# Instance norm on one core: the stores of the first two parts go from ScalarE's DMA queue to SyncE's

## The chip, the cores and the metric

The kernel runs on one core of one Trainium2 chip. The metric is device time in microseconds. Three runs of the kernel before took 1247.9, 1248.1 and 1248.12 us, median 1248.1. A core has five engines that matter here: TensorE (PE in the profile), VectorE (DVE), ScalarE (ACT), GpSimd (POOL) and SyncE (SP). SP and ACT each issue transfers on a hardware queue of their own; the profile names SP's queue q1 and ACT's q10. Both queues are worked off by the same 16 DMA engines.

## The reference

```python
# x: (8, 64, 32, 64, 64) float32, eps = 1e-5
mean = np.mean(x, axis=(2, 3, 4), keepdims=True)
var = np.var(x, axis=(2, 3, 4), keepdims=True)
return ((x - mean) / np.sqrt(var + eps)).astype(np.float32)
```

There are 512 instances (batch times channel) of 131072 float32 each, 268.4 MB in and as much out. Each instance is normalised by its own mean and variance.

## The kernel before

**Tiles and parts.** The input is one flat run of floats. A *part* is 128 partitions by 4096 floats, that is four whole instances, 2.1 MB, with 16 KiB in a partition. A *tile* is 128 by 12288 floats (three chunks of 4096), twelve instances, 6.3 MB, 48 KiB in a partition. The first two parts of the data (FRONT = 2) are done as parts, then come 41 tiles, then three more parts: 2 + 41 x 3 + 3 = 128 parts in all. Four slots of a tile's size hold the data (`slots[0]` to `slots[3]`); everything is computed in place in them.

**Where parts lie.** The two front parts use the first 4096 columns of slots 2 and 3, so the tile loads into slots 2 and 3 must wait until these parts have been stored. The three end parts lie side by side in slot 1, and are loaded when the store of tile 37, the last but three, has landed. The last tile, number 40, lies in slot 0.

**What is computed.** For a tile, VectorE and ScalarE sum the chunks, TensorE adds the sums over the partitions of an instance by a matrix of 1/131072 under a mask, a few small VectorE instructions (`over_instance`) put them together, and the same is done for the squares of the centred values; then VectorE scales two chunks and ScalarE one. For a part the same is done with one chunk, half of the elementwise work on each engine. The engines work through the parts and tiles in order: front parts, tiles, end parts (`over_tiles`). Each step is ordered by semaphores, one of each kind per slot or part ("lane"): `landed` (load done), `done` (scaled values ready), `stored` (store landed) are the ones that matter here.

**What sets the order of transfers.** There is no scheduler: each engine's instructions run in the order in which the code writes them, and one that waits holds up all that is behind it on the same engine.

- SP issues all loads (`load_all`): the two front parts, the tiles into slots 0 and 1, then those into slots 2 and 3, which wait for the stores of the first and second front part, then a loop over tiles 4 to 39 (line 391), each of which waits for the store of the tile four before it, then tile 40 (line 396) and the three end parts. Behind all of them SP stores tile 40 (line 402) and the three end parts (line 407).
- ScalarE issues the stores of tiles 0 to 39 (line 243) and, in the kernel before, those of the two front parts (line 310), each right behind the activation that finishes the data, in its own stream of instructions.

Which queue carries what, before: q1 has all loads, the last tile's store and the end parts' stores; q10 has the stores of the front parts and of tiles 0 to 39.

Of the kernel before, what the change touches and what calls it, by code (L numbers as in the profile page):

```python
# [9 lines left out]
def kernel(  # L10
# [26 lines left out]
    FRONT = 2  # L37
# [6 lines left out]
    out_f = out.rearrange("b c d h w -> (b c d h w)")  # L44
# [7 lines left out]
    def part_of(ap, m):  # L52
        first = (m if m < FRONT else m + THIRDS * n_tiles) * P * CHUNK
        return ap[first : first + P * CHUNK].rearrange("(p f) -> p f", p=P)
# [26 lines left out]
    def semaphores(name, n=LANES):  # L81
        return [ctx.enter_context(nc.semaphore(f"{name}{i}")) for i in range(n)]
# [11 lines left out]
    done = semaphores("done")  # L94
    stored = semaphores("stored")
# [188 lines left out]
            op1=Alu.add,  # L284
        )._wait_ge(shifted[lane], 1).then_inc(done[lane], 1)

    def part_on_scalar(eng, t, lane, dst):
        a, w = small[lane], CHUNK // 2
        eng.activation(  # L289
            out=unused[0][:, :w], in_=t[:, w:], func=Act.Identity, accum_out=a[:, 1:2]  # L290
        )._wait_ge(landed[lane], 16).then_inc(summed[lane], 1)
        eng.activation(  # L292
            out=unused[1][:],
            in_=t,
            func=Act.Square,
            bias=a[:, 2:3],
            accum_out=a[:, 3:4],
        )._wait_ge(centred[lane], 1).then_inc(squared[lane], 1)
        eng.activation(  # L299
            out=a[:, 5:6], in_=psum[lane][:, 2:3], func=Act.Sqrt, bias=eps_t[:, 0:1]  # L300
        )._wait_ge(varied[lane], 1).then_inc(rooted[lane], 1)
        eng.activation(  # L302
            out=t[:, :w],
            in_=t[:, :w],
            func=Act.Identity,
            scale=a[:, 6:7],
            bias=a[:, 7:8],
        )._wait_ge(shifted[lane], 1).then_inc(done[lane], 1)
        if dst is not None:
            eng.dma_start(out=dst, in_=t)._wait_ge(done[lane], 2).then_inc(  # L310
                stored[lane], 16
            )

    def part_on_tensor(eng, t, lane):
        a, p = small[lane], psum[lane]
# [9 lines left out]
    parts = [  # L325
        (SLOTS + m, slots[SLOTS - FRONT + m][:, :CHUNK], SLOTS - FRONT + m, 0)
        for m in range(FRONT)
    ]
# [14 lines left out]

    def over_tiles(eng, on_part, on_tile, with_target=False):
        def part(m):
            more = (part_of(out_f, m) if m < FRONT else None,) if with_target else ()
            on_part(eng, parts[m][1], parts[m][0], *more)

        for m in range(FRONT):
            part(m)  # L350
        counts = [
            ctx.enter_context(eng.register(f"{on_tile.__name__}_c{m}"))
            for m in (1, 3, 4, 16)
        ]
        for c, m in zip(counts, (1, 3, 4, 16)):
            eng.reg_mov(c, m)
        with eng.Fori(0, ROUNDS) as it:
            for s in range(SLOTS):
                more = (out_t[it * SLOTS + s],) if with_target else ()
                on_tile(eng, slots[s][:], s, *counts, *more)  # L360
            for c, m in zip(counts, (1, 3, 4, 16)):
                eng.reg_add(c, c, m)
        for k in range(ROUNDS * SLOTS, n_tiles):
            c = k // SLOTS + 1
            more = (out_t[k],) if with_target else ()
            if with_target and k == TAIL:
                more = (None,)
            on_tile(eng, slots[k % SLOTS][:], k % SLOTS, c, 3 * c, 4 * c, 16 * c, *more)
        for m in range(FRONT, n_parts):
            part(m)  # L370

    def load_all(eng):
        def part(m):
            lane, t, slot, uses = parts[m]
            load = eng.dma_start(out=t, in_=part_of(x_f, m))
            if uses:
                load._wait_ge(stored[slot], 16 * uses)
            load.then_inc(landed[lane], 16)

        for m in range(FRONT):  # L380
            part(m)
        for s in range(SLOTS):
            load = eng.dma_start(out=slots[s][:], in_=x_t[s])
            if s >= SLOTS - FRONT:
                load._wait_ge(stored[s + FRONT], 16)
            load.then_inc(landed[s], 16)
        c16 = ctx.enter_context(eng.register("load_c16"))
        eng.reg_mov(c16, 16)
        with eng.Fori(1, ROUNDS) as it:
            for s in range(SLOTS):  # L390
                eng.dma_start(out=slots[s][:], in_=x_t[it * SLOTS + s])._wait_ge(  # L391
                    stored[s], c16
                ).then_inc(landed[s], 16)
            eng.reg_add(c16, c16, 16)
        for k in range(ROUNDS * SLOTS, n_tiles):
            eng.dma_start(out=slots[k % SLOTS][:], in_=x_t[k])._wait_ge(
                stored[k % SLOTS], 16 * (k // SLOTS)
            ).then_inc(landed[k % SLOTS], 16)
        for m in range(FRONT, n_parts):
            part(m)  # L400
        s = TAIL % SLOTS
        eng.dma_start(out=out_t[TAIL], in_=slots[s][:])._wait_ge(
            done[s], 3 * (TAIL // SLOTS + 1)
        ).then_inc(stored[s], 16)
        for m in range(FRONT, n_parts):
            lane, t, _, _ = parts[m]
            eng.dma_start(out=part_of(out_f, m), in_=t)._wait_ge(done[lane], 2).then_inc(
                stored[lane], 16
            )

        for s in range(SLOTS):
            eng.wait_ge(stored[s], 16 * len(range(s, n_tiles, SLOTS)))
        for m in range(FRONT, n_parts):
            eng.wait_ge(stored[SLOTS + m], 16)

    def set_up(eng):
# [56 lines left out]
        return count  # L473

    load_all(nc.sync)
    set_by = set_up(nc.gpsimd)
    nc.vector.wait_ge(ready, set_by)
# [3 lines left out]
    nc.scalar.preload_act_table(Act.Sqrt)  # L481
    nc.scalar.wait_ge(ready, set_by)
    over_tiles(nc.scalar, part_on_scalar, tile_on_scalar, with_target=True)


# [33 lines left out]
```

## Time and profile before

| | |
|---|---|
| median of three runs | 1248.1 us (1247.9 to 1248.12) |
| the profiled execution, its own time | 1247.9 us |
| its span in the profile | 1246.2 us |
| moved | 536.9 MB, half in and half out, 431 GB/s over the span |
| VectorE busy | 804.6 us (65%) |
| ScalarE busy | 764.6 us (61%) |
| TensorE busy | 55.0 us (4%) |
| tile loads (41), median from issue to landing | 39.9 us |
| tile stores on ACT's queue (40), median from issue to landing | 54.2 us |
| part stores on ACT's queue (2), median | 27.9 us |
| part stores on SP's queue (3), median | 19.5 us |

The span is the stretch from the first to the last recorded instruction of the profiled execution; the time of an execution is some 1.7 us longer. A line of the timeline reads: start in us, length in us, engine, line of the code, operation, what is written and read, count, and in brackets the idle time before it and what ended that. An engine with a "q" (SPq, ACTq) is the engine's issuing of a transfer, not the transfer. "Issue to landing" runs from the issue of a DMA to the moment at which all 16 DMA engines have reported its data there; it holds the time that the transfer waits behind others on its queue.

### The profile page before, as it was taken

How to read it: one execution, taken by the hardware profiler on the slowest of the kernel's cores; microseconds unless marked ns; L12 is line 12 of the kernel's file. 1: busy time of each engine (PE TensorE's matmuls, PEld its weight loads, DVE VectorE, ACT ScalarE, POOL GpSimd, SP SyncE). 2: the span in 40 equal slices, each digit the busy share in tenths (PEclk: the TensorE clock that was granted, in tenths of full speed). 3: DMA queues.
4: the chain of work that ended last, by engine and by line, in shares of the span. 5: the costliest groups of instructions: out<-in, count | busy, mean ns of one | idle time of the engine just before them, and what ended most of it. 6: DMA issues, size and time to landing. Idle time of an engine off the chain costs nothing.

```text
span 1246.2 us, 1977 instructions
## 1 busy us (share of the span) xinstructions
PE 55.0 (4%) x184; PEld 46.1 (4%) x184; DVE 804.6 (65%) x722; ACT 764.6 (61%) x441; POOL 2.7 (0%) x15
## 2 busy tenths in 40 slices
PE   0000000000000000000000000000000000000000
PEld 0000000000000000000000000000000000000000
DVE  2887666666666666666666666666666666666661
ACT  5876555666566666655556665666566555566574
POOL 0000000000000000000000000000000000000000
DMA  9999999999999999999999999999999999999998
GB/s 395 429 429 439 440 429 432 431 426 448 432 429 429 432 443 435 429 431 432 440 439 429 429 432 437 442 431 429 431 431 448 432 429 429 432 442 439 430 422 368
DMA packets 13250, 536.89 MB, mean 431 GB/s; under 512 B 1472, under 2 KB 1472, under 8 KB 1472
## 3 DMA queue, kind: packets, MB, share of 16 engines
q1 hardware_dynamic: 7200, 281.02, 52.3%
q10 hardware_dynamic: 6048, 255.86, 47.4%
q14 instruction: 2, 0.02, 0.0%
HBM read 268.44 MB, written 268.44 MB: 431 GB/s over the span
## 4 chain that ended last, share of the span: by engine, by line
another core or an unknown queue 82%; DMA 9%; ACT 3%; DVE 2%; SPq 1%; issue 1%; PE 0%; ACTq 0%
DMA slot<-in_x_dram 6%; DMA out_dram<-slot 4%; ACT unused L222 1%; SPq L391 1%; ACT unused L292 1%; DVE small L159 0%; ACT unused L215 0%; DVE slot L202 0%; DVE slot L195 0%; ACT slot L302 0%; PE psum L253 0%; DVE small L266 0%; ACT unused L289 0%; PE psum L316 0%
## 5 line engine op out<-in xcount | busy, mean ns | idle before, releaser
L215 ACT ACTIVATE unused<-slot 128x4096 uint8<-128x4096 f32 x82 | 243.5, 2970 | 302.4 <-DMA slot<-in_x_dram 300.1
L159 DVE TENSOR_REDUCE small<-slot 128x1 f32<-128x4096 f32 x82 | 249.2, 3081 | 272.4 <-DMA slot<-in_x_dram 272.4
L222 ACT ACTIVATE unused<-slot,small 128x4096 uint8<-128x4096 f32 x82 | 303.5, 3703 | 63.6 <-DVE small L145 63.6
L173 DVE CUSTOM_DVE_ANT_0 unused<-slot 128x4096 uint8<-128x4096 f32 x41 | 181.5, 4426 | 1.4
L235 ACT ACTIVATE slot<-slot,small 128x4096 f32<-128x4096 f32 x41 | 155.9, 3802 | 18.1 <-DVE small L190 18.1
L202 DVE TENSOR_SCALAR slot<-slot,small 128x4096 f32<-128x4096 f32 x41 | 98.7, 2408 | 0.0
L253 PE MATMUL psum<-small,avg 128*128 128x9 f32 (+1 forms) x164 | 49.1, 375 | 1116.5 <-DVE small L127 1116.5
L166 DVE TENSOR_SCALAR slot<-slot,small 128x4096 f32<-128x4096 f32 x41 | 96.5, 2353 | 1.5
L195 DVE TENSOR_SCALAR slot<-slot,small 128x4096 f32<-128x4096 f32 x41 | 96.3, 2348 | 0.0
L253 PEld LDWEIGHTS psum<-small,avg 128*128 128x128 f32 x164 | 41.1, 311 | 1124.5 <-DVE small L127 1124.5
L133 DVE TENSOR_REDUCE small<-psum 128x3 f32<-128x12 f32 x82 | 13.9, 169 | 56.6 <-PE psum L253 56.6
L229 ACT ACTIVATE small<-small,eps_t 128x3 f32<-128x3 f32 x41 | 12.3, 300 | 61.2 <-DVE small L145 61.2
L127 DVE TENSOR_TENSOR small<-small,belongs 128x12 f32<-128x12 f32 x82 | 13.9, 170 | 31.3 <-ACT unused L222 28.9
L292 ACT ACTIVATE unused<-slot,small 128x4096 uint8<-128x4096 f32 x5 | 18.5, 3709 | 6.0 <-DVE small L269 6.0
L266 DVE TENSOR_REDUCE small<-slot 128x1 f32<-128x2048 f32 x5 | 11.4, 2283 | 10.8 <-DMA slot<-in_x_dram 10.8
L187 DVE RECIPROCAL small<-small 128x3 f32<-128x3 f32 x41 | 7.2, 176 | 15.0 <-ACT small L229 15.0
L272 DVE RECIPROCAL small<-small 128x1 f32<-128x1 f32 x5 | 0.8, 163 | 24.0 <-ACT small L299 24.0
L139 DVE TENSOR_TENSOR small<-small,belongs 128x9 f32<-128x9 f32 x82 | 14.0, 170 | 2.8
L222 ACT ACTIVATION_READ_ACCUMULATOR unused<-slot,small 128x1 f32 x82 | 15.4, 188 | 0.0
L215 ACT ACTIVATION_READ_ACCUMULATOR unused<-slot 128x1 f32 x82 | 15.4, 188 | 0.0
L145 DVE TENSOR_REDUCE small<-small 128x3 f32<-128x9 f32 x82 | 13.3, 162 | 2.8
L289 ACT ACTIVATE unused<-slot 128x2048 uint8<-128x2048 f32 x5 | 9.5, 1905 | 8.3 <-DMA slot<-in_x_dram 7.8
(26 smaller groups left out, 47.1 us busy)
## 6 DMA issues: line engine op xcount, KB each, us to landing
slot<-in_x_dram SPq DMA_DIRECT2D x41, 6144.0 KB, 39.9
out_dram<-slot ACTq DMA_DIRECT2D x40, 6144.0 KB, 54.2
slot<-in_x_dram SPq DMA_DIRECT2D x5, 2048.0 KB, 30.3
out_dram<-slot SPq DMA_DIRECT2D x1, 6144.0 KB, 31.7
out_dram<-slot SPq DMA_DIRECT2D x3, 2048.0 KB, 19.5
out_dram<-slot ACTq DMA_DIRECT2D x2, 2048.0 KB, 27.9
```

Source lines behind the costliest of these rows:

```text
L127: eng.tensor_tensor(out=block(a, by_both, n, m), in0=spread(a, at, m), in1=belongs[:, :, :m], op=Alu.mult,)._wait_ge(*wait).then_inc(steps ...
L139: eng.tensor_tensor(out=block(a, by_chunk, n, n), in0=spread(a, by_instance, n), in1=belongs[:, :, :n].rearrange("p i c -> p c i"), op=Alu ...
L159: eng.reduce_sum(out=column(a, SUMS, j), in_=part, axis=AXIS)._wait_ge(landed[lane], c16).then_inc(summed[lane], 1)
L166: eng.tensor_scalar(out=chunk[0], in0=chunk[0], scalar1=column(a, MEANS, 0), scalar2=None, op0=Alu.add,)._wait_ge(centred[lane], c1).then_ ...
L173: eng.tensor_tensor_reduce(out=unused[2][:], in0=chunk[0], in1=chunk[0], scale=1.0, scalar=0.0, op0=Alu.mult, op1=Alu.add, accum_out=colum ...
L195: eng.tensor_scalar(out=chunk[0], in0=chunk[0], scalar1=column(a, SCALES, 0), scalar2=None, op0=Alu.mult,)._wait_ge(scaled[lane], c1).then ...
L202: eng.tensor_scalar(out=chunk[1], in0=chunk[1], scalar1=column(a, SCALES, 1), scalar2=column(a, SHIFTS, 1), op0=Alu.mult, op1=Alu.add,)._w ...
L215: eng.activation(out=unused[j - 1][:, : part.shape[1]], in_=part, func=Act.Identity, accum_out=column(a, SUMS, j),)._wait_ge(landed[lane], ...
L222: eng.activation(out=unused[j - 1][:], in_=chunk[j], func=Act.Square, bias=column(a, MEANS, j), accum_out=column(a, SQUARES, j),)._wait_ge ...
L235: eng.activation(out=chunk[2], in_=chunk[2], func=Act.Identity, scale=column(a, SCALES, 2), bias=column(a, SHIFTS, 2),)._wait_ge(shifted[l ...
L253: eng.matmul(out=p[:, col : col + THIRDS * m], lhsT=avg[PART][:], rhs=a[:, at + m : at + m + THIRDS * m], start=True, stop=True,)._wait_ge ...
L292: eng.activation(out=unused[1][:], in_=t, func=Act.Square, bias=a[:, 2:3], accum_out=a[:, 3:4],)._wait_ge(centred[lane], 1).then_inc(squar ...
```

## The change

The stores of the two front parts leave ScalarE's instruction stream and are issued by SP. The store of the first front part stands right behind the load of slot 0, and that of the second right behind the load of slot 1. Each waits on SP until its part's `done` has reached two, as it did on ScalarE. Since SP runs in order, the load of slot 1 is now behind the wait of the first part's store, and the loads of slots 2 and 3 are behind that of the second. The end parts' stores use the same new helper, with the same place and the same waits as before. Nothing else moves: no computation, no size, no other wait changes. After it, q10 carries only the stores of tiles 0 to 39.

```diff
-    def part_on_scalar(eng, t, lane, dst):
+    def part_on_scalar(eng, t, lane):
...
-        if dst is not None:
-            eng.dma_start(out=dst, in_=t)._wait_ge(done[lane], 2).then_inc(
-                stored[lane], 16
-            )
...
     def over_tiles(eng, on_part, on_tile, with_target=False):
         def part(m):
-            more = (part_of(out_f, m) if m < FRONT else None,) if with_target else ()
-            on_part(eng, parts[m][1], parts[m][0], *more)
+            on_part(eng, parts[m][1], parts[m][0])
...
+        def store_part(m):
+            lane, t, _, _ = parts[m]
+            eng.dma_start(out=part_of(out_f, m), in_=t)._wait_ge(done[lane], 2).then_inc(
+                stored[lane], 16
+            )
+
...
         for m in range(FRONT):
             part(m)
         for s in range(SLOTS):
...
             if s >= SLOTS - FRONT:
                 load._wait_ge(stored[s + FRONT], 16)
             load.then_inc(landed[s], 16)
+            if s < FRONT:
+                store_part(s)
...
         for m in range(FRONT, n_parts):
-            lane, t, _, _ = parts[m]
-            eng.dma_start(out=part_of(out_f, m), in_=t)._wait_ge(done[lane], 2).then_inc(
-                stored[lane], 16
-            )
+            store_part(m)
```

## The prediction

> **What bounds the kernel now.** I read the page's slices first (is any engine or the DMA full), then the DMA queues, then stretches of the run, the DMA issues one by one at both ends, and last the timeline of the start and the end, where the change lies.
>
> The page: the DMA's busy tenths, its rate, and the two queues.
>
> ```profile
> DMA  9999999999999999999999999999999999999998
> GB/s 395 429 429 439 440 429 432 431 426 448 432 429 429 432 443 435 429 431 432 440 439 429 429 432 437 442 431 429 431 431 448 432 429 429 432 442 439 430 422 368
> ...
> q1 hardware_dynamic: 7200, 281.02, 52.3%
> q10 hardware_dynamic: 6048, 255.86, 47.4%
> ```
>
> The 16 DMA engines are full in every slice but the last, while VectorE and ScalarE are busy 65% and 61%. So the time is bytes over rate: 536.9 MB at 431 GB/s is 1246 us. Neither the bytes nor the packets change; only DMA idle time can be added or removed. Where is some? Stretches (length; busy of PE, weight load, VectorE, ScalarE, GpSimd; clock; DMA share; GB/s):
>
> ```profile
> 0.00:2.00 2.00, 0.00 (x0) 0.00 (x0) 0.00 (x0) 1.01 (x1) 1.04 (x7) 1.00 0.00 0
> ...
> 1000.00:1029.06 29.06, 1.20 (x4) 1.00 (x4) 19.14 (x17) 17.63 (x10) 0.00 (x0) 1.00 1.00 435
> ...
> 1235.00:1240.00 5.00, 0.00 (x0) 0.00 (x0) 0.00 (x0) 0.00 (x0) 0.00 (x0) 1.00 0.99 426
> 1240.00:1245.00 5.00, 0.00 (x0) 0.00 (x0) 0.00 (x0) 0.00 (x0) 0.00 (x0) 1.00 0.41 177
> ```
>
> Idle are the 2 us before the first packet and some 4 us at the very end. In between a tile (6.29 MB) goes each way in 29.0 us, so alone it takes 14.5 us and a part (2.10 MB) 4.85. The start and the end:
>
> ```profile
> 1.95 60.57 SPq L383 DMA_DIRECT2D slot<-in_x_dram  x4
> ...
> 19.30 0.38 ACTq L310 DMA_DIRECT2D out_dram<-slot  x1
> 19.74 1.91 ACT L289 ACTIVATE unused<-slot 128x2048 uint8<-128x2048 f32 x1 [0.47 <-ACT slot L302]
> ...
> 30.79 3.62 ACT L215 ACTIVATE unused<-slot 128x4096 uint8<-128x4096 f32 x1 [0.92 <-DMA slot<-in_x_dram]
> ...
> 52.69 0.36 ACTq L243 DMA_DIRECT2D out_dram<-slot  x1
> ...
> 91.48 29.33 SPq L391 DMA_DIRECT2D slot<-in_x_dram  x2
> ...
> 102.57 3.62 ACT L215 ACTIVATE unused<-slot 128x4096 uint8<-128x4096 f32 x1 [6.17 <-DMA slot<-in_x_dram]
> ```
>
> ```profile
> 1176.73 3.62 ACT L215 ACTIVATE unused<-slot 128x4096 uint8<-128x4096 f32 x1 [7.96 <-DMA slot<-in_x_dram]
> ...
> 1198.62 0.34 SPq L402 DMA_DIRECT2D out_dram<-slot  x1
> ...
> 1208.95 21.99 SPq L407 DMA_DIRECT2D out_dram<-slot  x3
> ```
>
> The part stores, us from issue to landing: first and second front part, then the last one of the end.
>
> ```profile
> out_dram<-slot ACTq DMA_DIRECT2D x1, 2048.0 KB, 23.5
> ...
> out_dram<-slot ACTq DMA_DIRECT2D x1, 2048.0 KB, 32.3
> ...
> out_dram<-slot SPq DMA_DIRECT2D x1, 2048.0 KB, 14.3
> ```
>
> A part store alone would need 4.85 us. The first front one lands at 19.3 + 23.5 = 42.8, the second at 29.9 + 32.3 = 62.2, so the second takes 19.4 = 4 x 4.85: beside a tile load it gets a quarter. That fits two queues served packet by packet, 16 KB for a part against 48 KB for a tile (row lengths 4096 and 12288 floats). Both landings matter: the slot 2 load waits for the first, the slot 3 load for the second (SP's two waits at the load line are 39.7 and 19.0 us).
>
> **The change, part by part, against this execution (span 1246.2, time 1247.9).**
>
> *ScalarE loses two issues.* 0.38 + 0.34 us; the next activation starts 0.44 us earlier (19.30, not 19.74), so the second part is done at 29.4 rather than 29.9. ScalarE waits 300 us for loads in all, so this is worth 0 in itself.
>
> *SP gains two issues with waits, ahead of the loads of slots 1, 2, 3.* Slot 1's load is now issued at 19.7 behind the first part's last activation, not at 2.4. Nothing is late by it if the queue still has work: part 0 lands at 8.8, part 1 at 13.7, slot 0, now alone, at 13.7 + 14.5 = 28.2 (30.8 before, when it shared). Cover 8.5 us, cost 0. The second store waits on SP until 29.4; behind it stand the loads of slots 2 and 3, which waited for the stores anyhow.
>
> *The order of transfers at the start.* One queue now runs them in sequence: slot 0 to 28.2; first part store to 33.1 (42.8 before); slot 1 to 47.6 (50.1); second part store to 52.5 (62.2). Slot 2's load is issued at 33.1 and slot 3's at 52.5, each before the queue runs dry. The queue never empties, so the DMA stays full: cost 0. Unknown is a gap where one queue turns from a store to a load, which no row before shows. Low end 0: at the end the last part load lands at 1216.0, the tile store behind it on the same queue at 1198.62 + 31.7 = 1230.3, 14.3 later, no gap. High end 3.0 each, the part of the first part load (7.8 us into an empty queue) that isn't its 4.85 of moving; four turns, 12 us. I take 0: a queued successor is what the row at the end has, an empty queue is not.
>
> *The phase that is left behind.* Tile 0 starts when ScalarE is free, 29.4, instead of 30.8; its store is issued at 51.3 (52.69). From 52.5 both queues hold whole tiles and share evenly: slot 2 lands at 52.5 + 29.0 = 81.5 (73.2 before), tile 0's store at about 81.9 (91.5), slot 3 at 110.5 (102.6). So loads run 8.0 us later and stores 9.6 earlier than before. Both queues stay filled: a store is issued 21.9 us after its load lands (1176.73 to 1198.62), e.g. tile 3's at 132.4, while tile 2's runs to 140; 7.5 us of backlog, where it was 25 (54.2 to landing less 29.0). Cost 0.
>
> *The end, where a later load does count.* The last tile's load lands at 1176.7 + 8.0 = 1184.7; counting bytes (loads 8.0 behind, stores 9.6 ahead do not cancel) it may be 1186.3; I take 1185.2. Its compute ends 21.9 later, 1207.1; the three parts end 10.33, 10.02 and 10.02 later (1198.62 to 1208.95; to 1230.6 from 1220.6): 1237.5, against 1230.6 before. Their loads are no limit: they wait for tile 37's store (1165.8 - 9.6 = 1156.2) and go at a quarter rate until the last whole store on the other queue lands at 1204.7, so they land near 1204.5, 1209.4, 1214.2. The load queue then stores the last tile to 1229, part A to 1234, part B to 1239. The last part store, issued 1237.5, no longer sits behind a queue for 14.3 us. It lands no earlier than bytes allow, 1244.9 as before, and no earlier than an issue into an empty queue, 1237.5 + 7.8 = 1245.3. So the 7 us that compute ends later eat the wait that the last store had, and leave +0.4.
>
> Sum: span 1246.2 + 0.4 = 1246.6; time 1247.9 + 0.4 = 1248.3; the shown runs' median lies 0.2 above this execution: 1248.5. What a measurement can tell from no change is about 0.2%, 2.5 us.
>
> The skill against the trace. Row: a part store on its own queue beside a tile load took 19.4 us, four times its share alone, and held slot 3's load back to 62.2. The Trainium skill, "DMA: Bandwidth & Descriptors", "Issuing engines are not separate DMA queues", says that the issuing engine does not matter but for sequencer time, since all run on the same 16 engines. By that alone the change is worth at most the 0.7 us of issues, 1247.4, and nothing shifts by 8 us; by the row phases shift, and the sum is 1248.5. The same page's "Queues, rings and completion order" has each engine go round its queues packet by packet, which is the row's side.
>
> **Rivals.**
>
> *A. Full DMA all along (forecast).* 1247.3 to 1249.8: the bound by bytes below, and a last load at 1186.3 above.
>
> *B. Gaps where the load queue turns between loads and stores.* Place: 28, 33, 48, 53 us, when the other queue is empty and can't fill in. For it: no row shows a store followed by a load on one queue. Against it: the turn at the end. From 0.6 us a turn it decides; 1 us gives 1248.5 + 4 = 1252.5. Slower.
>
> *C. The tail of computation becomes the bound.* The last load lands later than 1185.2, as when a queue runs dry at 7.5 us of backlog. For it: 1237.5 is only 1 us short of the previous store's end. Against: byte counting allows 1 us more. Every us beyond counts in full; from 1187.5 it decides, and 1189 gives 1252.3. Slower.
>
> *D. The end closes up.* DMA share 0.41 in the last 5 us shows that some engines trail. If they do not trail in the new order, bytes allow about 3 us less, but the compute chain must then end earlier too: 1245.3. Faster.
>
> *E. SP's wait ahead of slot 1's load starves the queue.* Decides only if the first part is done after 27; it was at 19.3. If at 30, +3: 1251.5.
>
> **How the numbers follow.** A 0.79, B 0.09, C 0.06, D 0.04, E 0.02. The time is A's. All of A and a share of B (gaps under 0.6 us) lie within 0.2%: 0.82; the rest of B, C and E are slower: 0.14; D faster: 0.04. For 8 in 10 the range takes A and the small gaps: 1246.8 to 1250.8.
>
> **What would show it.** Right: DMA at 9 tenths in every slice but the last; part stores at the front landing in some 14 and 23 us, issued by SP; tile 0's store at 51.3; the first steady load issue near 82 rather than 91.5; ScalarE's first wait for slot 3 ending near 110.5; last load landing near 1185; last part store issued near 1237.5 and landing in under 9 us. Wrong: a DMA share below 0.9 between 25 and 55 us (B, E), a last part done after 1240 (C), or a span under 1244 (D).

## The result and the profile after

The changed kernel takes 1397.0 us (median of four runs, 1393.1 to 1404.4) against 1248.1 us (median of four): 1.119 times as long, 95% interval 1.114 to 1.125. The forecast was 1248.5 us, range 1246.8 to 1250.8, no change. It is wrong by 148.5 us.

The page after: busy tenths of the DMA, its rate per slice, the two queues (packets, MB, share of the 16 engines).

```profile
span 1391.3 us, 1977 instructions
...
DMA  9999999899999999999999899999999999998957
GB/s 398 426 424 420 431 427 393 365 386 404 384 383 386 384 384 384 384 398 389 384 384 387 362 387 404 384 384 384 384 384 384 403 386 384 386 401 367 374 240 327
...
q1 hardware_dynamic: 7488, 285.22, 49.0%
q10 hardware_dynamic: 5760, 251.66, 44.3%
```

The packets moved as the change says: 288 packets and 4.2 MB from q10 to q1. The rate keeps near 425 for six slices and then sinks to some 384 for the rest of the run, although the DMA's row of tenths still reads 9 nearly everywhere. So the time is not in one place; every tile takes longer. Three stretches of two tiles' length of the kernel before (58 us each; the last columns are DMA share and GB/s):

```profile
300.00:358.00 58.00, 2.40 (x8) 2.00 (x8) 38.27 (x34) 35.26 (x20) 0.00 (x0) 1.00 1.00 434
600.00:658.00 58.00, 2.39 (x8) 2.00 (x8) 38.27 (x35) 35.26 (x22) 0.00 (x0) 1.00 1.00 434
900.00:958.00 58.00, 2.40 (x8) 2.00 (x8) 38.27 (x35) 35.26 (x21) 0.00 (x0) 1.00 1.00 434
```

and of the changed kernel:

```profile
300.00:358.00 58.00, 1.79 (x6) 1.50 (x6) 32.31 (x29) 29.98 (x19) 0.00 (x0) 1.00 0.95 393
600.00:658.00 58.00, 1.80 (x6) 1.50 (x6) 32.82 (x27) 29.87 (x16) 0.00 (x0) 1.00 0.93 381
900.00:958.00 58.00, 2.40 (x8) 2.00 (x8) 33.61 (x33) 31.44 (x19) 0.00 (x0) 1.00 0.97 397
```

A share of 0.95 with a rate of 393 instead of 434 says two things: some DMA time is idle, and some packets take longer than before (393 over 0.95 is 414 GB/s of busy time, less than 434). The timeline of the changed kernel, start and end:

```profile
19.32 0.34 SPq L377 DMA_DIRECT2D out_dram<-slot  x1
...
33.96 19.80 SPq L386 DMA_DIRECT2D slot<-in_x_dram  x2
...
51.05 0.39 ACTq L243 DMA_DIRECT2D out_dram<-slot  x1
...
87.30 1146.77 SPq L396 DMA_DIRECT2D slot<-in_x_dram  x36
1266.33 0.34 SPq L401 DMA_DIRECT2D slot<-in_x_dram  x1
...
1331.53 3.62 ACT L215 ACTIVATE unused<-slot 128x4096 uint8<-128x4096 f32 x1 [11.44 <-DMA slot<-in_x_dram]
...
1353.42 0.34 SPq L407 DMA_DIRECT2D out_dram<-slot  x1
...
1363.74 20.37 SPq L377 DMA_DIRECT2D out_dram<-slot  x3
```

Where the 145.1 us of span come from: the load of tile 4 is issued at 87.3 (91.5 before), 4.2 us earlier. The 36 tile periods from there to the load of tile 40 take 1179.0 us, 32.75 each; before it was 1045.3, 29.04 each: +133.7. From that issue to the end it is 125.0 instead of 109.4: +15.6, of which the load itself takes 25.3 more and everything behind its landing 9.7 less.

**What the trace shows below the views.** Each of the 16 DMA engines reports the landing of its 8 of the 128 rows by itself. The 16 reports of slot 2's load, of tile 0's store and of the two transfers after them, in us, sorted, in the changed kernel:

```
load  tile 2  79.6 79.6 79.7 79.7 79.7 79.8 79.9 79.9 79.9 79.9 80.0 80.2 80.4 80.7  86.2  87.1
store tile 0  83.3 83.3 83.3 83.3 83.3 83.4 83.4 83.4 83.5 83.6 83.6 83.8 84.1 84.3  86.4  87.3
load  tile 3 108.6 108.6 108.7 108.7 108.8 108.8 108.8 108.9 108.9 108.9 109.0 109.2 109.8 110.5 119.4 121.5
store tile 1 112.2 112.2 112.3 112.3 112.4 112.4 112.4 112.4 112.5 112.5 112.6 112.7 113.3 113.9 119.6 121.7
```

(The times are counted from the profile's zero; some expectations below give the same landings up to 0.5 us earlier or later.) Two engines lose 6 to 7 us in the first tile in which both queues carry whole tiles, and 4 to 6 more in the next. Later they are some 44 us behind the others (tile 20's load: by 635.7 us on the 14, 677.5 and 680.1 on the two), and since a load waits for all 16 engines' part of a store, the other 14 wait for the two. In the kernel before the last engine was 0.8 to 2.4 us behind the first in every load, and at most 3.4 in a store.

What is different on these two? The packet records around tile 0's store, summed up (start, length in us, queue):

```
first packets of slot 2's load    52.08 to 53.05, 1.81 each, q1, 16 engines
second packets of slot 2's load   53.89 to 54.36, 1.81 to 2.13, q1, 14 engines
first store packets               54.72 2.11 q10 and 54.86 2.09 q10, two engines
first store packets               55.73 to 56.49, 1.81 each, q10, 14 engines
```

Tile 0's store reached the engines between 54.4 and 54.7. Fourteen had begun the second load packet and went on load, load, store, load, store. Two had begun their first load packet 0.4 to 1 us after the others and were just ending it (at 54.72 and 54.86), and went load, store, load, store: there the store of row i follows the load of row i. If an engine takes the 8 rows of a load and of a store in the same order, which the trace does not show, the two are on the same SBUF partition, in different slots. I call that *in step*. The landings tell it apart: on the two late engines the store lands 0.2 us behind the load, on the others 3.6, one load packet plus one store packet (a pair). The offset below is the landing of a tile's store less that of the load two tiles on, in pairs of 3.63 us; a tile has 8 pairs.

Packets of 48 KiB that took longer than 1.85 us between 300 and 600 us of each profile (store packets over 2.2 us in brackets):

| kernel | loads | stores | offset of load and store, in pairs |
|---|---|---|---|
| before | 0 of 1323 | 0 of 1331 (0) | 5 |
| changed | 417 of 1212 | 288 of 1154 (163) | 0 on two engines |

The two engines carry only some 150 packets of each kind in that time. So packets on the other 14 are long too: around 600 us these no longer alternate, but take the eight store packets of a tile, then eight load packets, and wait.

### The profile page after: what moved, and what is told of

Read it like the earlier page. It is cut to its first block, busy times and chain, and to the rows that moved or that the text cites. A ratio compares the mean times of both kernels' runs of the same rounds, so it can differ in the third digit from the quotient of the medians.

```text
span 1391.3 us, 1977 instructions
## 1 busy us (share of the span) xinstructions
PE 55.0 (4%) x184; PEld 46.0 (3%) x184; DVE 804.5 (58%) x722; ACT 764.0 (55%) x441; POOL 2.7 (0%) x15
## 4 chain that ended last, share of the span: by engine, by line
DVE 35%; another core or an unknown queue 31%; ACT 26%; PE 4%; issue 3%; DMA 1%; DVEq 0%; ACTq 0%; SPq 0%
ACT unused L222 22%; DVE small L159 17%; DVE slot L202 7%; DVE slot L195 5%; PE psum L253 4%; ACT unused L292 1%; DVE small L139 1%; DVE small L127 1%; DVE small L133 1%; DVE small L145 1%; ACT small L229 1%; ACT unused L215 1%; ACT slot L302 1%; DMA slot<-in_x_dram 1%
```

## The experiments

Four theories: *step* (an engine on which store row i follows load row i is slow, wherever the part stores are issued), *queue* (SP's queue must not carry stores between its loads), *backlog* (7 us of waiting stores are too few), and later *weak engines* (two engines of the chip are slow by themselves).

### One part only

```diff
 # e1, e12: the first part's store on SP, the second's on ScalarE
+            if s == 0:
+                lane, t, _, _ = parts[s]
+                eng.dma_start(out=part_of(out_f, s), in_=t)._wait_ge(done[lane], 2)...
 # e2: the second part's store on SP, the first's on ScalarE
+            if s == 1:
+                (the same)
```

> Only the first front part's store is issued by SP, the second one's stays on ScalarE. Theory step: in the changed kernel two of the 16 DMA engines lose some 6 us in the first tile in which both queues are full (landings of slot 2's load at 79.4 to 80.4 us on 14 engines and 86.0 and 86.8 on two), because on them the first packet of tile 0's store came in right behind the first packet of slot 2's load (load, store, load, store) and on the others one packet later (load, load, store, load). What counts is where tile 0's store falls in slot 2's load. Here the bytes at the front go in another order but end at nearly the same time (second part store near 45 instead of 53, slot 1's load near 53 instead of 48), so the two meet within a packet again: 1330 to 1400 us, if the store does not fall past the first packet by chance. Theory queue: the time is lost because SP's queue carries stores between its loads; with one such store instead of two, slower than before, between 1250 and 1400. Theory backlog: the store queue holds only 7 us of work instead of 25 and cannot bridge; backlog is as in the changed kernel, 1370 to 1400.

> Only the second front part's store is issued by SP, the first one's stays on ScalarE. Theory step: slot 2's load begins on the DMA engines at the same time as in the changed kernel (the same bytes stand ahead of it), near 52, but tile 0's store is issued near 52.6 instead of 51.05, because ScalarE is held up as in the kernel before; so it comes in during the second packet of slot 2's load, on all 16 engines: no engine falls behind, 1248 to 1253 us. Theory queue: a store stands among SP's loads: slower, 1320 to 1400. Theory backlog: stores run 8 to 9 us ahead of before, loads 8 us behind, as in the changed kernel: 1370 to 1400.

> Only the first front part's store on SP, once more, timed: one look gave 1259.6, with slot 2's load landing 3.6 us (one load and one store packet) ahead of tile 0's store on all engines. Theory step: a store that follows the load of the next row, not of its own, costs little: 1255 to 1265 again, and no engine falls back by several us per tile. Theory queue: between 1250 and 1400, as the one look does not show the spread.

Measured: the first part alone 1259.6 us in one execution, and 1260.7 (1258.6 to 1264.6) in six more, 1.0073 times the kernel before [1.0045, 1.0102]. The second part alone 1251.7 us, 1.0006 [0.9987, 1.0026]; of its eleven executions the profiled one was the longest, 1261.8, so its landings are not those of a typical one.

The first landings are 3.6 us apart with the first part (slot 2's load 79.7 to 81.1, tile 0's store 83.3 to 85.0) and 7 us with the second (77.7 to 80.7 and 84.1 to 86.6): about one pair and two pairs. No engine falls back by several us per tile. The first expectation for the first part was too high in its main case, 1330 to 1400; the store fell past the first packet there. Neither part alone is 12%, and the queue theory has no place for 0.06%. The backlog theory falls with the second part: loads and stores are nearly as far from those of before as in the changed kernel. One pair costs a little: 225 of 1310 load packets between 300 and 600 us took over 1.85 us, no store packet.

### The changed kernel with tile 0 later, and the changed kernel again

```diff
 # e6, in the ScalarE stream ahead of tile 0
+            eng.activation(out=unused[1][:, :4096], in_=avg (broadcast), func=Act.Identity)...
+            eng.wait_ge(late, 1)      # late: that activation is done
 # e5: no edit
```

> The changed kernel once more, beside the three below on the same chip. Theory step says that whether an engine falls behind hangs on a fraction of a microsecond between tile 0's store and slot 2's load, so another chip may give another time; then anything from 1250 to 1400. Theory queue and theory backlog: 1390 to 1405 on every chip.

> The changed kernel with one more ScalarE activation (4096 columns of the constant matrix into the scratch buffer, some 3.7 us) ahead of tile 0, so that tile 0's store is issued about two packets of 1.82 us later than in the changed kernel. Theory step: no engine takes the load and the store of the same row one after the other; 1248 to 1255 us, and at least 100 us below the changed kernel where that is at 1390. Theory queue: as the changed kernel, 1390. Theory backlog: as the changed kernel or worse, 1390 or more.

Measured side by side: the changed kernel again 1399.8 us, 1.1165 times before [1.1126, 1.1204]; with tile 0 later 1252.1 us, 1.0004 [0.9988, 1.0020]. The rate per slice with tile 0 later:

```profile
GB/s 382 435 428 436 436 432 428 431 440 437 428 431 436 442 428 431 432 443 428 431 432 440 431 431 434 440 429 431 434 442 429 429 436 442 429 428 437 430 433 324
```

Both part stores are on SP's queue and all waits for transfers are as in the changed kernel; the added activation moved the issue of tile 0's store from 51.0 to 55.1 us. It takes 148 us away. Load and store land 10.9 us apart then, three pairs, and 11 of 1315 load packets and no store packet exceed 1.85 us. The queue theory falls here, and the backlog theory a second time. In the repeat of the changed kernel five engines were late in the first tile (slot 2's load at 86.4 to 88.1, the others 79.8 to 82.8), so their number varies; three of the five left the step between tiles 15 and 21.

### Slot 2's load one wait later

```diff
 # e4: the changed kernel, in load_all
+            if s == SLOTS - FRONT:
+                eng.wait_ge(stored[SLOTS + FRONT - 1], 16)
```

> The changed kernel, but slot 2's load also waits on SP for the second part's store, so that it is issued at 53.4 instead of 34 and its first packet starts some 2 us after that, near 55, behind the first packet of tile 0's store on all 16 engines (store, load, store, load, in the same order on each). Theory step: the relation is the same on all engines, so their landings stay within 3 us of each other; whether a store packet right ahead of the load packet of its own number also costs is open: 1250 if not, 1390 with all engines late if so. Theory queue: 1390 to 1400, two engines late. Theory backlog: 1390 to 1400.

Measured: 1263.2 us in one execution. The phase settled at one pair (landings 3.6 us apart), as with the first part alone, and so did the time. An order of store first did not stay, since the load came two packets late, so whether that order costs with stores from SBUF was not seen.

### In HBM, in the partition's addresses, in half stores

```diff
 # e7: tile stores at another pitch in the output
+    out_t = out_f[...].rearrange("(p k f) -> k p f", p=P, f=COLS)
 # e11: scratch buffers between the slots
+        slots.append(sbuf(f"slot{s}", [P, COLS]))
+        if s < THIRDS:
+            unused.append(sbuf(f"unused{s}", [P, CHUNK], mybir.dt.uint8))
 # e8: two stores of 64 partitions for one of 128
+            for h in (0, P // 2):
+                eng.dma_start(out=dst[h : h + P // 2], in_=t[h : h + P // 2])...
     # ... and 32 for 16 where these stores are waited for
```

> The changed kernel, but tile stores go to other places of the output: row p of tile k is written to row p x 41 + k, not k x 128 + p, so the rows of the output are exchanged; bytes, packets, queues, waits and partitions are the same. It asks where two packets in step meet. If it is in HBM (load and store addresses at a fixed distance), that distance now differs from row to row: 1250 to 1300. If it is in SBUF (the load writes the partition that the store reads), nothing changes: as the changed kernel beside it, 1390 if that is slow. If rows 1.97 MB apart are themselves slow to write, stores are slow on all engines: above 1400.

> The changed kernel with the three 4 KiB scratch buffers laid between the four slots, so that the columns of the load and of the store of one tile pair lie 104 KiB apart in their partition instead of 96. If the meeting of a load and a store costs by their addresses inside the partition, 1250 to 1300; if it costs by the partition or by the order of the packets alone, 1390 to 1405.

> The changed kernel, but each whole tile is stored by two transfers of 64 partitions, one behind the other; packets stay 48 KiB, 8 per engine and tile, and the phase of the queues is the same, but an engine's store packet is mostly of another partition than its load packet. Theory step with a meeting in SBUF or in HBM rows: few pairs of the same row, 1250 to 1290. Theory queue and theory backlog: 1390 to 1400.

Measured, one execution each: other output addresses 1399.6 us, other spacing of the slots 1396.9 us. Both have two late engines in the first tile (slot 2's load at 87.6 and 87.8; 88.0 and 88.1), like the changed kernel. So a fixed distance of the two rows in HBM is not what it takes, nor is the distance of 96 KiB inside a partition. The half stores took 1496.5 us, against every theory: all 16 engines were slow and their order was lost (375, 370 and 376 GB/s in the three stretches). All 16 engines read the same 64 partitions there, so it is no clean test of another partition, and why it is the slowest stays open.

### All engines in step

```diff
 # e9: the changed kernel, one extra store ahead of slot 2's load
+            if s == SLOTS - FRONT:
+                eng.dma_start(
+                    out=part_of(out_f, n_parts - 1)[:, :960], in_=parts[1][1][:, :960]
+                ).then_inc(extra, 16)
+            if s == SLOTS - 1:
+                eng.wait_ge(extra, 16)
```

> The changed kernel with one small extra store (128 x 960 floats, 0.5 MB) on SP's queue between the second part's store and slot 2's load, so that slot 2's load starts some 1.1 us later on every DMA engine, and tile 0's store comes in behind its first packet on all 16 (load, store, load, store). Theory step: the engines that stay up with 79 to 80 us in the changed kernel fall behind too: slot 2's load lands after 85 us on most of the 16, and with all of them slow alike the time is 1380 or more. Rival theory weak engines: two engines of a chip are slow whenever the queues are this close, the others not: slot 2's load lands near 81 on 14 and 87 or later on two, 1390. Theory queue: the same two late engines, 1390.

Measured: two executions, and they differ: the profiled one took 1437.5 us, the other 1258.3. I read the profiled one for what it shows inside, not for a typical time. Its rate:

```profile
GB/s 394 406 377 385 377 378 372 381 371 370 371 368 374 366 370 368 371 377 379 372 375 367 372 374 375 375 378 375 378 383 382 386 371 385 377 385 374 374 332 325
```

Slot 2's load lands at 86.6 us or later on 14 of the 16 engines; tile 4's load lands at 152.2 to 156.4 on 14, and tile 2's store 0.2 us behind it. Between 300 and 600 us 573 of 1130 store packets take over 2.2 us, half of them, where the changed kernel has a seventh. So more than two engines can be slow, as in the repeat with five and in the next experiment with all 16: the weak engines theory falls. That the same program ran in 1258.3 as well fits a phase that hangs on parts of a microsecond, but the other execution has no trace to show it.

### The kernel before, brought into step

```diff
 # e10 and e13: the kernel before
+            if s == SLOTS - FRONT:
+                eng.wait_ge(stored[SLOTS + FRONT - 1], 16)
 # e10 only
+            eng.activation(out=unused[1][:, :3072], in_=avg (broadcast), func=Act.Identity)...
```

> The kernel before, with the part stores on ScalarE's queue as they were, but its queues brought near step: slot 2's load also waits for the second part's store (issue near 53.5 instead of 42.8), and one more ScalarE activation of 3072 columns ahead of tile 0 puts tile 0's store near 55.7. Theory step: where the two first packets meet, the loss comes without any store on SP's queue: 1330 to 1400 if the aim is true on at least one engine; if they miss by more than a packet, 1250 to 1270, and the landings of slot 2's load and tile 0's store show by how much. Theory queue: SP's queue has only loads: 1250 to 1260 in any case.

> The kernel before with one wait more and nothing else: slot 2's load also waits for the second part's store. All part stores at the front stay on ScalarE's queue. In the run with the added activation slot 2's first load packets ran from 54.1 to 56.6 us on all 16 DMA engines and the store of tile 0, issued at 55.2, came in two packets too late. Without the activation the store is issued near 52.7 and comes in near 55.5 to 56, while the first load packet runs: load, store, load, store with equal row numbers on nearly all engines. Theory step: 1380 to 1440, with nearly all engines slow, as in the 1437 us execution of the run with the extra store. Theory queue: SP's queue carries no store at the front: 1248 to 1256.

Measured: with the activation 1256.1 us in one execution; the aim was off (load 81.7 to 84.6, store 88.0 to 90.0, 7 us apart in the middle). Without it 1422.7 us (median of four, 1396.1 to 1433.7) against 1249.0 of the kernel before on the same chip, 1.139 times; the two shortest alone, 1396.1 and 1415.3, give 1.1247 [1.1154, 1.1339]. All part stores at the front are on ScalarE's queue. The three stretches of the execution of 1433.7:

```profile
300.00:358.00 58.00, 1.74 (x6) 1.44 (x6) 29.73 (x26) 26.91 (x15) 0.00 (x0) 1.00 0.99 366
600.00:658.00 58.00, 1.79 (x6) 1.50 (x6) 29.69 (x28) 27.39 (x16) 0.00 (x0) 1.00 0.99 374
900.00:958.00 58.00, 2.40 (x8) 2.00 (x8) 34.19 (x34) 31.18 (x18) 0.00 (x0) 1.00 0.99 369
```

The DMA is full here, share 0.99, and yet moves only 366 to 374 GB/s: with all engines in step nobody waits, the packets are long (544 of 1131 store packets between 300 and 600 us over 2.2 us). This is the kernel before plus one wait, and the same wait with the added activation took 1256.1, so it is not the wait: the phase alone is enough for the whole loss. The way there was not the one expected: tile 0's store came in first, and tile 1's still landed some 3.6 us ahead of tile 3's load; all 16 were in step from tile 4's load (145.6 to 148.6, tile 2's store 145.8 to 148.8) to tile 29's. Tile 2 landed at 89.3 and its store was issued at 111.2, 22 us later, when the store queue was running dry (tile 1's landed at 110.0 to 112.7), and tile 3's load landed at 113.6 to 114.7: both queues began a new tile together.

### Stores that do not read SBUF

```diff
 # e14: the kernel of the 1422.7 us; e15: the kernel before; both with the output pitch of e7
-            eng.dma_start(out=dst, in_=t)._wait_ge(done[lane], c3)...
+            eng.dma_start(out=dst[0], in_=dst[1])._wait_ge(done[lane], c3)...   # dst[1]: the tile in the input
```

> The kernel before with the wait that brought its queues into step (1422 us), but the tile stores read their rows from the input in HBM instead of the slot in SBUF (rows of the output at the pitch that changed nothing in the changed kernel); the output is then a copy of the input for the tiles, the normalised values are not stored. Theory step in SBUF: what costs is a store that reads the partition that the load before it has just written; with no SBUF read there is nothing to meet, and the time is that of the same copies out of step (the run beside this one) within 1%, near 1250. Rival step by packet order alone: 1390 to 1430 as with stores from SBUF, at least 8% above the run beside this one.

> The kernel before, out of step as it is, with the same copies from HBM in the place of the tile stores: the price of such copies by themselves. If they move at the 1.82 us per 48 KiB packet of a store, 1248 to 1256; if they are slower or faster, this run says by how much, and the run beside it is read against it.

Measured: with the wait 1257.2 us, 1.0064 times before [1.0029, 1.0100]; without it, the control, 1272.9 (two executions), 1.0185 [1.0133, 1.0237]. The stretches with the wait:

```profile
300.00:358.00 58.00, 2.40 (x8) 2.01 (x8) 38.27 (x35) 35.26 (x21) 0.00 (x0) 1.00 1.00 434
600.00:658.00 58.00, 2.40 (x8) 2.01 (x8) 38.23 (x35) 35.22 (x21) 0.00 (x0) 1.00 1.00 434
900.00:958.00 58.00, 2.40 (x8) 2.01 (x8) 38.26 (x34) 35.25 (x20) 0.00 (x0) 1.00 1.00 434
```

Load and store land 0.2 us apart from tile 2 to the end, but not in the same order throughout. Up to tile 10 the store lands 0.2 us ahead of the load on all 16 engines (84.0 to 85.5 for tile 2's load, 83.9 to 85.4 for tile 0's store): the packets go store, load, store, load, so this is not yet the order of the changed kernel, and the first stretch does not test it. From tile 11 on engines pass over to load, store, load, store, with the store 0.2 us behind the load: seven have that order in the second stretch and eight in the third. There they run at full rate: the last packets of tiles 30 and 28, around 898 us, take 1.81 us on all eight but for one of 2.03, and the third stretch moves 434 GB/s. In the changed kernel two such engines were enough for 12%. So the order of packets alone costs nothing; the loss needs stores that read SBUF beside loads that write it. The control was slower than the run with the wait by 1.2%, just outside the 1% that was expected; I can't explain it, and it does not bear on this reading, since both are far from 1422.

## Why the prediction was wrong

- **The front's timetable was right.** Predicted and measured: first part's store issued 19.3 and 19.3; slot 2's load issued 33.1 and 34.0; slot 1's load landed 47.6 and 48.5; second part's store landed 52.5 and 53.4; tile 0's store issued 51.3 and 51.05. No gap of 3 us appeared where the queue turns between loads and stores: DMA share 0.97 and 418 GB/s from 27 to 52 us, more than the 0.93 and 402 of the kernel before. Rival B did not happen, nor did E. The next signs in time failed: the first steady load was issued at 87.3, not near 82, and slot 3's load landed at 121.5, not near 110.5.
- **The step that failed is "the phase that is left behind", with "Cost 0".** It says that from 52.5 both queues hold whole tiles and share evenly, and puts the cost of a shift of the two against each other at nothing. The even sharing was right on the 14 engines. But the cost of a packet was taken from the kernel before, where the store of a row and the load of the same row were 5 pairs apart, and carried over to a phase that no row of that profile showed. What the runs showed in its place: on two engines a tile each way took 32.6 us instead of 29.0, the others waited for them, and 36 tile periods grew by 133.7 us. I put the loads 8.0 us later and the stores 9.6 earlier, 17.6 together: worked out in pairs of 3.63 us that is 4.9, from five pairs to none. The numbers for "in step" stood in the prediction, slot 2's load landing at 81.5 and tile 0's store at 81.9, and I read them as harmless. The unknown should have been bounded from both sides there, as it was for the turns of the queue.
- **The bound was misread as bytes over rate.** It held that neither bytes nor packets change, so only idle time counts. The rate itself fell from 434 to between 381 and 397 GB/s, in part by longer packets, in part because 14 engines waited for two.
- **The end was right in itself.** The chain from the last load's landing to the last part store's issue was worked out as 52.3 us and took 52.2 (1331.53 to 1383.78); the last store landed 6.2 us after its issue, against 7.8 taken. It is the one large gain: 9.7 us behind the last load.
- **Rival C** (a tail of computation) and **D** did not decide. C's sign, a later last load, was there, at 1331.5 instead of 1185, but the place was every tile and not the end.
- **The skill's rule against the row.** The Trainium skill, "DMA: Bandwidth & Descriptors", "Issuing engines are not separate DMA queues", says that the issuing engine matters only for sequencer time. For the queue as such the runs agree: both part stores on SP, three pairs out of step, 1.0004 times before. The shift of phases that the row of 19.4 us foretold is what made the 12%.

How the time went with the phase, from the runs whose whole tiles are stored from SBUF in one transfer. The offset is that of the profiled execution, and the times come from several chips, on which the kernel before took what the last row says:

| offset of load and store of a row | kernels | time, us |
|---|---|---|
| 0 on nearly all engines | before plus one wait; extra store (profiled execution; the other took 1258.3) | 1422.7; 1437.5 |
| 0 on some engines | changed, its repeat, other addresses, other spacing | 1397 to 1400 |
| 1 pair | first part alone; slot 2's load later | 1260.7; 1263.2 |
| about 2 pairs | second part alone (its profiled execution 1261.8); before plus wait and activation | 1251.7; 1256.1 |
| 3 pairs | changed with tile 0 later | 1252.1 |
| 5 pairs (of 8) | before | 1248 to 1253 |

Shown is that the loss follows the phase (a delay of one activation takes it away, one wait brings it to the kernel before) and needs stores that read SBUF. That the meeting is on one partition is argued from the rows (0 pairs against 1), not shown: a store in step with a load, at the same rate, but from other partitions, was not had, and the half stores, which were expected to read mostly other partitions than the loads write, were slow as well. Open are also the half stores themselves and the 1258.3 us execution. That two engines met the store at a packet's end and 14 did not hung on less than 1 us, which the prediction could not have resolved; that a meeting is possible could be read from its own 81.5 and 81.9.

## What to carry to other kernels

Where a kernel is bound by its DMA and streams equal tiles in and out on two queues, the phase of the two is part of the schedule: look at whether each store packet comes right behind the load packet of the same row, and keep the two apart. Here three and five load-and-store pairs cost nothing and two nothing clear of the noise (1.0006), one pair cost 0.7%; four, six and seven were not run. A full DMA row in tenths does not say that the rate is the best one; read GB/s per tile beside it, and the landings engine by engine. An edit that costs nothing on its own may still move the phase, so a delay of a few us is worth trying before the edit is judged.

## What the runs showed of the hardware that was not expected

- A load and a store of 48 KiB per row, in step, take some 2.0 us a packet and more instead of 1.81: the late engines in the changed kernel need 32.6 us for the 16 packets of a tile each way, where the kernel before needs 29.0. With all 16 in step (the execution of 1433.7 us, 300 to 600 us) loads averaged 2.07 us and stores 2.15.
- The state lasts. In the changed kernel two engines stay in step from tile 2 to the last; I read it from the order of waits, by which the next load and store of such a pair are both in their queues before it ends. It can be left: in the repeat five engines became two by tile 21, and in the kernel before plus one wait 16 became nine by the last tile.
- One engine's delay is every engine's: 2 of 16 engines, at 32.6 us a tile instead of 29.0, made the tile period 32.75 us and the kernel 11.9% slower.
- Stores of 64 partitions, two in the place of one of 128, with packets of the same size and number, made the changed kernel 1496.5 us (one execution), against 1397.
